# Background products of w_mod queued on VectorE behind the weight splits traced before them

## The chip, the cores and the metric

The kernel runs on one core of a Trainium2 chip, in one launch. The metric is the device time in microseconds. The engines are TensorE (PE, its weight loads PEld), VectorE (DVE), ScalarE (ACT) and SyncE (SP, here the queue that issues the transfers); GpSimd (POOL) does next to nothing. Each engine runs its own queue in order, and waits on semaphores where an instruction needs another engine's result or a transfer.

## The reference, cut to what matters

Two layers over 256 tokens of width 2048, all in float32. Each layer normalises, modulates by a vector that comes from `c`, projects, runs two mixing branches, merges them and projects back. The part that the change touches is the product of the modulation, a row times a matrix of 2048 x 6144 in each layer:

```python
c_act = jax.nn.silu(c)
...
mod = c_act @ w_mod + b_mod
shift, scale, gate = jnp.split(mod, 3, axis=-1)
h = rms_norm(x, g_norm) * (1.0 + scale[:, None, :]) + shift[:, None, :]
proj = h @ w_in
...
y_ret = (o_ret * jax.nn.silu(rg)) @ w_ret_proj
...
y_mla = (o_mla * jax.nn.silu(mg)) @ w_mla_proj
...
out = merged @ w_out
return x + gate[:, None, :] * out
```

## The kernel before, in words

**Weights.** Every weight matrix is streamed once from memory in loads of 512 KB (128 partitions x 1024). A load lands in one of five staging buffers (`wst`, pool `wp`, WP = 5; `load`, line 237, issued on SP). To keep float32 accuracy with the faster matmul, each weight is split into two parts: `split_into` lets ScalarE write the rounded part `hi` (line 241) and VectorE the rest `lo` = source minus `hi` (line 242). Both go into one of three buffers (`whl`, pool `hp`, HP = 3). `chunk` (line 264) then runs the matmuls of this load: two for each block with `hi` (line 270), and after these one with `lo` (line 273). A staging buffer is free when its split has ended; a `whl` buffer is free when the matmuls of its load have ended. `load_split` (line 246) traces load and split, the split with a priority of 200 ahead of its place (SPLITS).

**The modulation.** The product with `w_mod` runs on VectorE: for every 128 rows of `w_mod` one instruction multiplies a block of 128 x 512 by one column of `cact` and adds it to an accumulator (`mod_rows`, lines 344 and 346). It is cut into pieces of one load, thus two such instructions (a pair), and these pieces wait in the list `background`. `load_split` calls `bg()` ahead of its own load; `bg()` adds `rate` to a credit and traces a piece for each whole credit. A piece is traced in one of two ways. `mod_pair` (line 391), for the first products of a layer, loads into two buffers of its own (`ring`, RING = 2) and adds into two accumulators `tmp`; it runs from 45 to 275 us and from 1110 to 1235. `mod_slice` (line 405) loads into the weights' staging buffers and adds into `macc`; there are 64 such pieces in layer 0 (439 to 950 us) and 32 in layer 1 (1477 to 1865). The rates: 0.85 and 0.76 a load in the first products; in layer 0 then 0.6 (RB, branch products, up to 590 us), 0.3 (RM, attention, 600 to 800) and 0.5 (RG, output gates, up to 950); in layer 1 0.3 throughout (BG1). After the last piece of a block of 512 columns `mod_finish` cuts the sum into three bf16 pieces (ScalarE line 362, VectorE 363) that small matmuls add up over the partitions (line 352).

**The order of the work.** The kernel is traced in Python, and a planner gives each engine its queue when the trace is done. It goes by priority (the place in the trace, less what `high_priority` takes off) and by its own estimate of when an instruction can start. So the order on an engine is not the order of the trace: a product whose transfer the planner takes to have landed goes ahead of a split whose buffer it takes to be busy still. The names that matter are `split_into`, `load_split`, `mod_rows`, `mod_pair` and `mod_slice`.

Of the kernel before, what the change touches and what calls it, by code (L numbers as in the profile page):

```python
# [9 lines left out]
F32 = mybir.dt.float32  # L10
# [4 lines left out]
ALU = mybir.AluOpType  # L15
# [93 lines left out]
def trunk(ctx: ExitStack, tc: tile.TileContext, x, c, positions, w_mod, b_mod, g_norm, w_in, g_cq,  # L109
          g_ckv, w_uq, w_ukv, w_ret_proj, w_mla_proj, w_out, g_final, consts, decay, out):  # L110
    nc = tc.nc
    V, A, T, DMA = nc.vector, nc.scalar, nc.tensor, nc.sync
# [17 lines left out]
    def tmp_tile():  # L130
        return tp.tile([P, 512], F32, name="tmp", tag="tmp")
# [101 lines left out]
    def load(src, nk, n):  # L233

        t = wp.tile([P, 1024], F32, name="wst", tag="wst")
        v = t[:, : nk * n].rearrange("p (k n) -> p k n", k=nk)
        DMA.dma_start(v, src.rearrange("(k p) n -> p k n", p=P))
        return v

    def split_into(hi, lo, src):  # L240
        A.activation(hi, src, AF.Copy)  # L241
        V.tensor_tensor(lo, src, hi.bitcast(F32), ALU.subtract)  # L242

    prepared = []

    def load_split(src, nk, n, early=False):
        if prepared and not early:
            return prepared.pop(0)
        bg()
        w = load(src, nk, n)  # L250
        t = hp.tile([P, 2, 1024], F32R, name="whl", tag="whl")
        hi = t[:, 0, : nk * n].rearrange("p (k n) -> p k n", k=nk)
        lo = t[:, 1, : nk * n].rearrange("p (k n) -> p k n", k=nk)
        with tc.high_priority(offset=SPLITS):
            split_into(hi, lo, w)
        return hi, lo

    def mm3(o, a, b, start, stop):
# [22 lines left out]
    def proj(w, col, n, act, span=(0, KT)):  # L281
        accs = [acc_tile() for _ in range((n + 2 * P - 1) // (2 * P))]
        nk = 1024 // n
        for k0 in range(*span, nk):
            hi, lo = load_split(w[k0 * P : (k0 + nk) * P, col : col + n], nk, n)
            proj_chunk(accs, hi, lo, k0, nk, span, act)
        return accs

    def proj_tok(w, col, act, span=(0, KT)):

        accs = [acc_tile() for _ in range(2)]
        for k0 in range(*span, 2):
            hi, lo = load_split(w[k0 * P : (k0 + 2) * P, col : col + 512], 2, 512)
            chunk([(accs[t].rearrange("p a b -> p (a b)"), (hi[:, k, :], lo[:, k, :]),
                    act.block(k0 + k, slice(t * P, (t + 1) * P)), k0 + k == span[0], k0 + k == span[1] - 1, True)
                   for k in range(2) for t in range(2)])
        return [a.rearrange("p a b -> p (a b)") for a in accs]
# [41 lines left out]
    macc = cp.tile([P, 512], F32, name="macc")  # L339

    def mod_rows(acc, w, k0, nk):
        for k in range(nk):
            if k0 + k == 0:
                V.tensor_scalar(acc, w[:, k, :], cact[:, 0:1], None, ALU.mult)
            else:
                V.scalar_tensor_tensor(acc, w[:, k, :], cact[:, k0 + k : k0 + k + 1], acc, ALU.mult, ALU.add)  # L346
# [10 lines left out]
    def mod_finish(l, m0, ng, acc):  # L357

        t1, t2 = (tp.tile([P, 2, 512], BF16, name="part", tag="tmp") for _ in range(2))
        pieces = [t[:, : ng * P] for t in (t1[:, 0], t1[:, 1], t2[:, 0])]  # L360
        for i in range(2):
            A.activation(pieces[i], acc, AF.Copy)
            V.tensor_tensor(pieces[2] if i else acc, acc, pieces[i], ALU.subtract)
        if l < DEPTH - 1 or m0 < 32:
            mod_sum(l, m0, ng, pieces, ones_h[:, 0:1])
            return
        b, n = tmp_tile(), m0 - 32
        DMA.dma_start(b, b_mod[l, m0 * P : m0 * P + 512].unsqueeze(0).broadcast_to([P, 512]))
        if n % 8 == 0:
            gate_row.append(quarter("grow"))  # L370
        ps = aux_tile()
        for i, piece in enumerate(pieces):
            T.matmul(ps, ones_h, piece, start=i == 0, stop=i == 2)
        V.tensor_tensor(gate_row[n // 8][:, n % 8 * P : n % 8 * P + 512], ps, b, ALU.add)

    rings, used = [], [0]

    def ring():
        if not rings:
            rings.extend(quarter("ring") for _ in range(RING))  # L380
        return rings

    def mod_fetch(w, l, m0, k0, ng):

        n = ng * P
        w = w.rearrange("p (k n) -> p k n", n=n)
        nd = 1024 // n
        DMA.dma_start(w, w_mod[l, k0 * P : (k0 + nd) * P, m0 * P : m0 * P + n].rearrange("(k p) n -> p k n", p=P))
        return w

    def mod_pair(l, kg, ng):

        acc = [tmp_tile()[:, : ng * P] for _ in range(2)]
        nd = 8 // ng
        for k0 in range(0, KT, nd):
            for i in range(2):
                room = ring()
                used[0] += 1
                mod_rows(acc[i], mod_fetch(room[used[0] % len(room)], l, kg + 16 * i, k0, ng), k0, nd)
                yield  # L400
        for i, a in enumerate(acc):
            mod_finish(l, kg + 16 * i, ng, a)
        make_amul(l, kg, ng)

    def mod_slice(l, m0, k0):
        w = load(w_mod[l, k0 * P : (k0 + 2) * P, m0 * P : m0 * P + 512], 2, 512)
        mod_rows(macc, w, k0, 2)
        if k0 + 2 == KT:
            mod_finish(l, m0, 4, macc)

    def make_amul(l, k, n):
        V.scalar_tensor_tensor(amul[l][:, k : k + n], mods[l][:, 16 + k : 16 + k + n], 1.0,
                               gn[l][:, k : k + n], ALU.add, ALU.mult)
# [4 lines left out]
    def bg():  # L418
        credit[0] += rate[0] if background else 0
        while background and credit[0] >= 1:  # L420
            credit[0] -= 1
            background.pop(0)()
# [12 lines left out]
    def make_h(l, k, xh, hh):  # L435

        t = tmp_pair()
        for i in range(2):
            scale, shift = amul[l][:, k + i : k + i + 1], mods[l][:, k + i : k + i + 1]
            A.activation(t[:, i], xh[:, i], AF.Identity, bias=shift, scale=scale)  # L440
        split_into(*hh.pair(k // 2), t)
# [52 lines left out]
    def start():  # L494
# [8 lines left out]
        with tc.manual_schedule(engines={ENG.PE, ENG.DVE, ENG.Activation}):  # L503
# [32 lines left out]
            for k in range(ng):  # L536
                V.tensor_scalar(xh0[:, k, :], xh0[:, k, :], amul[0][:, k : k + 1], None, ALU.mult)
            first = [w_in[0, k0 * P : (k0 + 2) * P, n : n + 512] for n in (C_RQ, C_RK) for k0 in range(0, ng, 2)]
            prepared.append(load_split(first[0], 2, 512, early=True))
            mod_sum(0, 0, ng, [acc], ones[:, 0:1])  # L540
            for k in range(ng):
# [7 lines left out]
    def scaled(l, n):  # L549


        w = S + 2
        tiles = [quarter("u", F32R) for _ in range((2 * n + 2) // 3)]
        parts = [tiles[i // 3][:, i % 3 * w : (i % 3 + 1) * w] for i in range(2 * n)]
        for k in range(n):
            t = tmp_tile()[:, :w]
            V.tensor_scalar(t[:, :S], xT[:, k, :], amul[l][:, k : k + 1], None, ALU.mult)
            V.tensor_copy(t[:, S:], mods[l][:, k : k + 1].broadcast_to([P, 2]))
            split_into(parts[2 * k], parts[2 * k + 1], t)
        return parts  # L560
# [426 lines left out]
    def queue(l, lo, hi):  # L987
        for m in range(lo, hi, 4):
            for k0 in range(0, KT, 2):
                background.append(lambda l=l, m=m, k0=k0: mod_slice(l, m, k0))  # L990
# [26 lines left out]
```

## Time and profile before

| | |
|---|---|
| median of 3 runs | 2107.25 us (2105.28 to 2107.37) |
| the profiled execution | 2107.54 us, of which the span from the first to the last instruction is 2105.8 us |
| mean granted TensorE clock | 0.993 of full speed |
| TensorE matmuls busy | 97% of the span |
| VectorE busy | 72% |
| ScalarE busy | 50% |
| read from memory | 456 MB, 218 GB/s over the span with what is written |

Times in the rows below are microseconds from the span's start. A busy share is a mean over stages, so the stages are looked at one by one. A line such as `DVE macc L346` is VectorE writing the tile `macc` at line 346 of the kernel; `<-DMA wst<-in_w_mod` names what ended the idle time before it. Idle time of an engine counts only if TensorE or the end of the kernel waits for it in turn.

### The profile page before, as it was taken

The numbers are of one execution on the slowest core, as the hardware profiler recorded it, in microseconds if no ns is written. First come the engines' busy times: TensorE is split into PE (matmuls) and PEld (weight loads), VectorE is DVE, ScalarE is ACT, GpSimd is POOL, SyncE is SP. The second block draws the span as 40 slices with busy tenths as digits, with TensorE's granted clock in tenths as the row PEclk, the third lists the DMA queues.
The fourth block names the chain that finished last, engine by engine and source line by source line (L and its number), as shares of the span: only waits on it lengthen the run. The fifth ranks groups of instructions, "written<-read, shape, count | busy, mean of one in ns | idle before, by whom it ended". The sixth has DMA issues, their size and how long they took to land. (4 is left out here: it accounts for less than half of the span.)

```text
span 2105.8 us, 31895 instructions
## 1 busy us (share of the span) xinstructions
PE 2045.3 (97%) x12410; PEld 1806.7 (86%) x12414; DVE 1505.9 (72%) x2258; ACT 1060.1 (50%) x1489; POOL 0.2 (0%) x4
## 2 busy tenths in 40 slices
PE   7999999999999999999999999999999999999998
PEld 4887888997789998778999779889878999988887
DVE  5789887777777786666577776557866777765564
ACT  4554355654356665334454454446544666644453
POOL 0000000000000000000000000000000000000000
PEclk9999999999999999999999999999999999999999
DMA  8988866566766667776558976665667666666672
GB/s 315 310 283 274 293 190 199 165 196 228 263 203 194 186 196 250 242 242 216 181 167 304 313 256 184 196 186 156 196 220 231 184 193 186 216 221 189 192 243 91
DMA packets 263511, 460.60 MB, mean 219 GB/s; under 512 B 18464, under 2 KB 68032, under 8 KB 263360
## 3 DMA queue, kind: packets, MB, share of 16 engines
q1 hardware_dynamic: 263360, 458.57, 68.4%
q8 instruction: 97, 1.59, 0.3%
q14 instruction: 54, 0.44, 0.1%
HBM read 456.41 MB, written 2.10 MB: 218 GB/s over the span
## 5 line engine op out<-in xcount | busy, mean ns | idle before, releaser
L241 ACT ACTIVATE whl<-wst 128x1024 fp32r<-128x1024 f32 (+1 forms) x708 | 706.9, 1006 | 770.4 <-PE acc L273 634.9
L242 DVE TENSOR_TENSOR whl<-wst,whl 128x1024 fp32r<-128x1024 f32 (+1 forms) x708 | 811.6, 1156 | 267.2 <-ACT whl L241 264.0
L270 PE MATMUL acc<-whl,h 128*128 128x512 f32 x2048 | 513.6, 391 | 0.9 <-DVE rv L606 0.7
L270 PEld LDWEIGHTS acc<-whl,h 128*128 128x128 f32 x2048 | 381.6, 188 | 79.8 <-issue 1.7
L270 PE MATMUL acc<-h,whl 128*128 128x256 f32 x2432 | 331.0, 287 | 8.6 <-ACT h L241 3.8
L270 PEld LDWEIGHTS acc<-h,whl 128*128 128x128 f32 x2432 | 310.0, 194 | 12.5 <-ACT h L241 5.0
L273 PE MATMUL acc<-whl,h 128*128 128x512 f32 x1024 | 281.8, 395 | 8.5 <-DVE whl L242 8.1
L270 PE MATMUL acc<-whl,z 128*128 128x512 f32 x1024 | 256.7, 392 | 3.8 <-ACT whl L241 3.8
L346 DVE SCALAR_TENSOR_TENSOR macc<-wst,cact,macc 128x512 f32<-128x512 f32 x180 | 135.0, 750 | 140.9 <-DMA wst<-in_w_mod 138.8
L273 PEld LDWEIGHTS acc<-whl,h 128*128 128x128 f32 x1024 | 188.8, 188 | 53.9 <-DVE whl L242 16.9
L270 PEld LDWEIGHTS acc<-whl,z 128*128 128x128 f32 x1024 | 192.8, 189 | 44.7 <-ACT whl L241 4.5
L273 PE MATMUL acc<-h,whl 128*128 128x256 f32 x1216 | 175.1, 284 | 0.0
L273 PEld LDWEIGHTS acc<-h,whl 128*128 128x128 f32 x1216 | 159.1, 193 | 0.1
L273 PE MATMUL acc<-whl,z 128*128 128x512 f32 x512 | 139.8, 395 | 13.2 <-DVE whl L242 13.1
L346 DVE SCALAR_TENSOR_TENSOR tmp<-ring,cact,tmp 128x512 f32<-128x512 f32 x150 | 112.0, 751 | 51.4 <-DMA ring<-in_w_mod 49.9
L273 PEld LDWEIGHTS acc<-whl,z 128*128 128x128 f32 x512 | 95.2, 189 | 39.2 <-DVE whl L242 20.3
L270 PE MATMUL acc<-c,whl 128*128 128x256 f32 x640 | 102.7, 289 | 1.0 <-DVE ma L643 1.0
L270 PEld LDWEIGHTS acc<-c,whl 128*128 128x128 f32 x640 | 86.8, 191 | 1.3 <-ACT q L241 1.2
L270 PE MATMUL acc<-m,whl 128*128 128x256 f32 x512 | 67.3, 283 | 0.0
L270 PEld LDWEIGHTS acc<-m,whl 128*128 128x128 f32 x512 | 64.0, 192 | 0.1
L270 PE MATMUL acc<-whl,m 128*128 128x512 f32 (+1 forms) x256 | 56.5, 365 | 0.0
L273 PE MATMUL acc<-c,whl 128*128 128x256 f32 x320 | 56.0, 283 | 0.0
(259 smaller groups left out, 1889.7 us busy)
## 6 DMA issues: line engine op xcount, KB each, us to landing
wst<-in_w_in SPq DMA_DIRECT2D x416, 512.0 KB, 4.5
wst<-in_w_mod SPq DMA_DIRECT2D x96, 512.0 KB, 4.3
ring<-in_w_mod SPq DMA_DIRECT2D x80, 512.0 KB, 5.5
wst<-in_w_ret_proj SPq DMA_DIRECT2D x64, 512.0 KB, 4.8
wst<-in_w_mla_proj SPq DMA_DIRECT2D x64, 512.0 KB, 4.6
wst<-in_w_out SPq DMA_DIRECT2D x64, 512.0 KB, 3.7
wst<-in_w_ukv SPq DMA_DIRECT2D x32, 512.0 KB, 3.8
wst<-in_w_uq SPq DMA_DIRECT2D x32, 384.0 KB, 4.0
```

The costliest lines, as they stand in the source:

```text
L241: A.activation(hi, src, AF.Copy)
L242: V.tensor_tensor(lo, src, hi.bitcast(F32), ALU.subtract)
L270: T.matmul(o, x, y, start=start and i == 0, stop=False, skip_group_check=True)
L273: T.matmul(o, x, y, start=False, stop=stop, skip_group_check=True)
L346: V.scalar_tensor_tensor(acc, w[:, k, :], cact[:, k0 + k : k0 + k + 1], acc, ALU.mult, ALU.add)
```

## The change

`split_into` hands back its VectorE instruction, and `load_split` keeps it in the list `last_split`. `behind_splits()` gives a context in which every VectorE instruction that is traced gets an edge to the split that was traced last. The edge is an order in VectorE's queue at planning time; it is no semaphore. Both places that trace background products, `mod_pair` and `mod_slice`, trace `mod_rows` in that context. The loads of `w_mod` are outside of it, and so is `mod_finish`. The products in `start()`, at the head of the kernel, stay as they are.

```diff
--- before.py
+++ after.py
@@ -239,9 +239,13 @@
 
     def split_into(hi, lo, src):
         A.activation(hi, src, AF.Copy)
-        V.tensor_tensor(lo, src, hi.bitcast(F32), ALU.subtract)
-
-    prepared = []
+        return V.tensor_tensor(lo, src, hi.bitcast(F32), ALU.subtract)
+
+    prepared, last_split = [], []
+
+    def behind_splits():
+
+        return tc.issue_after(last_split[-1].ins) if last_split else nullcontext()
 
     def load_split(src, nk, n, early=False):
         if prepared and not early:
@@ -252,7 +256,7 @@
         hi = t[:, 0, : nk * n].rearrange("p (k n) -> p k n", k=nk)
         lo = t[:, 1, : nk * n].rearrange("p (k n) -> p k n", k=nk)
         with tc.high_priority(offset=SPLITS):
-            split_into(hi, lo, w)
+            last_split.append(split_into(hi, lo, w))
         return hi, lo
 
     def mm3(o, a, b, start, stop):
@@ -396,7 +400,9 @@
             for i in range(2):
                 room = ring()
                 used[0] += 1
-                mod_rows(acc[i], mod_fetch(room[used[0] % len(room)], l, kg + 16 * i, k0, ng), k0, nd)
+                w = mod_fetch(room[used[0] % len(room)], l, kg + 16 * i, k0, ng)
+                with behind_splits():
+                    mod_rows(acc[i], w, k0, nd)
                 yield
         for i, a in enumerate(acc):
             mod_finish(l, kg + 16 * i, ng, a)
@@ -404,7 +410,8 @@
 
     def mod_slice(l, m0, k0):
         w = load(w_mod[l, k0 * P : (k0 + 2) * P, m0 * P : m0 * P + 512], 2, 512)
-        mod_rows(macc, w, k0, 2)
+        with behind_splits():
+            mod_rows(macc, w, k0, 2)
         if k0 + 2 == KT:
             mod_finish(l, m0, 4, macc)
```

## Rows read from the trace of the kernel before

**Rows 1.** Page, part 1: engine, busy us, share of the span, instructions

```profile
PE 2045.3 (97%) x12410; PEld 1806.7 (86%) x12414; DVE 1505.9 (72%) x2258; ACT 1060.1 (50%) x1489; POOL 0.2 (0%) x4
```

**Rows 2.** Waits: who waited for whom: us in total, times, longest us

```profile
DVE macc L346 <- DMA wst<-in_w_mod: 138.8, 74, 6.3
```

**Rows 3.** Windows by stage: length, busy us (x instructions) by engine, TensorE clock, DMA

```profile
500.00:600.00 100.00, 90.47 (x453) 74.24 (x453) 72.83 (x104) 36.15 (x42) 0.00 (x0) 0.95 0.75 246
600.00:800.00 200.00, 198.91 (x1659) 197.42 (x1658) 156.01 (x308) 129.34 (x256) 0.00 (x0) 1.00 0.64 193
850.00:965.00 115.00, 105.29 (x483) 81.92 (x484) 77.30 (x93) 44.21 (x50) 0.00 (x0) 1.00 0.74 243
1610.00:1868.00 258.00, 255.97 (x1946) 246.57 (x1947) 193.73 (x356) 157.03 (x291) 0.00 (x0) 1.00 0.65 200
```

**Rows 4.** Timeline, VectorE, 865 to 877: start, us, instruction [idle before <- releaser]

```profile
865.02 2.35 DVE L242 TENSOR_TENSOR whl<-wst,whl 128x1024 fp32r<-128x1024 f32 x2
870.50 1.54 DVE L346 SCALAR_TENSOR_TENSOR macc<-wst,cact,macc 128x512 f32<-128x512 f32 x2 [3.12 <-DMA wst<-in_w_mod]
871.95 1.22 DVE L242 TENSOR_TENSOR whl<-wst,whl 128x1024 fp32r<-128x1024 f32 x1
876.06 0.75 DVE L346 SCALAR_TENSOR_TENSOR macc<-wst,cact,macc 128x512 f32<-128x512 f32 x1 [2.89 <-DMA wst<-in_w_mod]
```

**Rows 5.** Timeline, the same stretch, ScalarE and TensorE

```profile
865.73 1.06 ACT L241 ACTIVATE whl<-wst 128x1024 fp32r<-128x1024 f32 x1 [3.67 <-PE acc L273]
...
878.00 1.20 PE L273 MATMUL acc<-whl,z 128*128 128x512 f32 x4 [1.76 <-DVE whl L242]
```

**Rows 6.** Timeline, VectorE: first and last pair of macc, and their splits

```profile
445.15 0.48 DVE L344 TENSOR_SCALAR macc<-wst,cact 128x512 f32<-128x512 f32 x1
...
452.71 1.22 DVE L242 TENSOR_TENSOR whl<-wst,whl 128x1024 fp32r<-128x1024 f32 x1
...
1862.92 1.54 DVE L346 SCALAR_TENSOR_TENSOR macc<-wst,cact,macc 128x512 f32<-128x512 f32 x2 [4.31 <-DMA wst<-in_w_mod]
...
1867.86 2.35 DVE L242 TENSOR_TENSOR whl<-wst,whl 128x1024 fp32r<-128x1024 f32 x2
```

**Rows 7.** Timeline, TensorE: transposes that end an output block, layers 0 and 1

```profile
851.15 0.87 PE L895 MATMUL aux<-cst,tmp 128*128 128x128 f32 x6
...
903.28 0.88 PE L895 MATMUL aux<-cst,tmp 128*128 128x128 f32 x6
...
1967.04 0.81 PE L895 MATMUL aux<-cst,tmp 128*128 128x128 f32 x6
...
2011.47 0.82 PE L895 MATMUL aux<-cst,tmp 128*128 128x128 f32 x6
```

**Rows 8.** Timeline of VectorE, ScalarE, TensorE, 499 to 506; window 505 to 513

```profile
499.73 0.75 DVE L346 SCALAR_TENSOR_TENSOR macc<-wst,cact,macc 128x512 f32<-128x512 f32 x1 [1.43 <-DMA wst<-in_w_mod]
...
503.19 0.21 ACT L302 ACTIVATE small<-small 128x4 f32<-128x4 f32 x1 [4.07 <-DVE small L745]
...
505.34 3.78 PE L270 MATMUL acc<-whl,z 128*128 128x512 f32 x8 [3.54 <-ACT whl L241]
...
505.00:513.00 8.00, 6.05 (x14) 4.26 (x15) 7.34 (x12) 0.44 (x2) 0.00 (x0) 0.50 0.66 233
```

**Rows 9.** Waits of matmuls (PE) and weight loads (PEld), 500 to 600

```profile
PE acc L273 <- DVE whl L242: 5.0, 4, 1.6
...
PEld acc L273 <- DVE whl L242: 7.4, 6, 2.3
```

**Rows 10.** Waits of weight loads, 1477 to 1610

```profile
PEld acc L273 <- DVE whl L242: 4.4, 3, 1.8
```

**Rows 11.** Timeline, VectorE, 99 to 110: a split, the first group's last products

```profile
99.37 1.22 DVE L242 TENSOR_TENSOR whl<-wst,whl 128x1024 fp32r<-128x1024 f32 x1
...
108.72 1.54 DVE L346 SCALAR_TENSOR_TENSOR tmp<-ring,cact,tmp 128x512 f32<-128x512 f32 x2 [0.31 <-DMA ring<-in_w_mod]
```

**Rows 12.** Page, part 6: issues, KB each, median us to landing

```profile
wst<-in_w_mla_proj SPq DMA_DIRECT2D x64, 512.0 KB, 4.6
```

## The prediction

> **What bounds the kernel now.** I read the busy table first: TensorE is busy for 2045.3 of 2105.8 us, VectorE for 72%, ScalarE for 50% [rows 1]. So the kernel is as long as TensorE's work plus what TensorE waits, and a change that moves VectorE's work can only win or lose TensorE's waits. Next the list of waits: the longest wait of VectorE that isn't for a weight half of ScalarE is that of the products of w_mod (line 346) for their own transfer, 138.8 us in 74 waits [rows 2]. Then the table by stage, to find where TensorE loses: 9.5 us of 100 in the stage 500 to 600 and 9.7 of 115 in 850 to 965, but only 1.1 of 200 and 2.0 of 258 in the two attention stages [rows 3]. Those first two are the stages in which a product is traced before every second load or more (rates 0.6 and 0.5).
>
> The timeline shows the two joined. VectorE runs its queue in order. Two splits end at 867.4; next in the queue is a product of w_mod, and VectorE stands 3.12 us until that transfer has landed and runs the pair of products (1.54 us); only then, at 871.95, comes a weight split [rows 4]. The other half of that weight had been written by ScalarE at 865.73 plus 1.06, so the split could have run from 866.8: it lost 5.1 us to a product [rows 5]. The next split waits in the same way behind a product that stood 2.89 us and began at 876.06 [rows 4], and TensorE stands 1.76 us for that split until 878.00 [rows 5].
>
> Does the change reach these products? Loads go out on SP in the order in which they are traced, and the splits run in that order too, so I numbered them: for each of the 96 pairs of products that share the weights' five staging buffers I counted the splits that were traced before the pair but run after it. 92 of 96 pairs have at least one, most two or three: the first pair begins at 445.15, while the split traced last before it runs at 452.71; the last pair runs at 1862.92, its split (the first of the two merged) at 1867.86 [rows 6]. The change forbids just that.
>
> **The change, part by part.** No instruction, transfer or semaphore is added or taken away; 92 pairs of 1.54 us move behind one to three splits of 1.22 us on VectorE. The loads of w_mod keep their place on SP's queue. What follows from a move is the release of the product's staging buffer, and so the load five places on, and the loads behind that one on SP.
>
> *Stage 850 to 955* (rate 0.5). The same work runs in layer 1 without products, so I price it by the period from one set of output transposes to the next: 903.28 - 851.15 = 52.1 us here (the next period is as long), 2011.47 - 1967.04 = 44.4 us there [rows 7]. The difference is 7.7 us a period, 15.4 us in two; a part of it is the small matmuls of a finished block, which stay. A chunk of one load needs 2.72 us of TensorE (44.4 less some 0.9 for the eight transposes, over 16), and its split needs 1.22 of VectorE, the products 0.77 on the mean: once in order, nothing on VectorE is late by its length. I take 12 of 15.4, leaving some for landings that are late by themselves. A rule of the Trainium skill bears on this price: the page Perfetto Trace Analysis, section Identifying the Most-Contended Engine, says that matmul busy time is no good measure of how near to its limit TensorE is, since matmuls overlap in the trace. By busy time the stage has only 9.7 us to give; by the period 15.4. The trace agrees with the rule, as the period sets the same work with products against the same without.
>
> *Stage 500 to 600* (rate 0.6). TensorE waits 5.0 us for splits by its own idle time and 7.4 by that of the weight loads [rows 9]. Beside it stands one other wait: ScalarE stood 4.07 us until 503.19 for statistics (line 745) on VectorE, the weight copies behind it came late, and TensorE stood 3.54 us until 505.34; after it the granted clock was 0.50, the lower of its two levels (1.2 GHz), from 505 to 513 [rows 8]. TensorE is busy for 6.05 us of that stretch at half speed, so 3.0 lost. Sum 5.0 + 3.5 + 3.0 = 11.5 to 7.4 + 3.5 + 3.0 = 13.9. The product at 499.73, which stood 1.43 us for its transfer in front of those statistics [rows 8], goes behind the split it overtook, so the statistics come some 2 us sooner; whether 3.5 us shrink enough for the clock to hold is open. I take 10.
>
> *Stage 1477 to 1610* (layer 1, rate 0.3): the weight loads wait 4.4 us for splits [rows 10]. I take 3.
>
> *Attention stages* (600 to 800 and 1610 to 1868): 3.1 us of waits altogether [rows 3]. Here a pair overtakes up to five splits and moves far, so the sign is open: the gain is at most 3.1, the loss is bounded below as a rival. I take 1.5 won.
>
> *First products of each layer* (45 to 330, 1100 to 1260), where products read two buffers of their own. There most pairs already run behind the split that they will be tied to: the last of the first group is traced before load 22 (16 products at 0.85 a load are 19 calls, and three loads were prepared without one), whose predecessor's split is at 99.37, and it runs at 108.72 [rows 11]. Of 80 such pairs I count 21 that overtake a split, mostly one split by half a pair. Their stalls for their own transfers stay in the queue ahead of splits. I take 1.5, with -2 to +4 as bounds, and 0.5 for the rest.
>
> Sum: 12 + 10 + 3 + 1.5 + 1.5 + 0.5 = 28.5 us. The profiled execution took 2107.54 us (span 2105.8 and 1.7 around it), 0.3 above the median of 2107.25; 2107.5 - 28.5 = **2079 us**. If all is won the terms are 15.4 + 13.9 + 4.4 + 3.1 + 4 + 0.5 = 41.3, so 2066.
>
> **What could take the place of the wait.** *The five staging buffers bind.* A load holds a buffer from its issue to the end of its split or pair. Five buffers and 1.5 loads for each chunk allow a mean hold of 5 x 2.72 / 1.5 = 9.1 us at full speed (8.5 at rate 0.6). Now the chunk takes 52.1 / 16 = 3.26 us, hence a mean hold of 10.9. After: a landing of 4.6 us [rows 12], then 1.06 and 1.22 with 0.1 between each are 7.1 us for a weight; a pair must outlast the split before it, whose load is issued no later, so at most 7.1 + 1.5 = 8.6. Mean 7.6 to 7.7, with 0.8 to 1.5 to spare. If queues on ScalarE and VectorE add 2.5 us to each, the hold is 10.1, the chunk 3.0 us, and some 0.25 x 32 = 8 us are won in the 850 stage and 4 elsewhere: 2095 us. In its favour: a product now leaves its buffer before the weights, and will hold it longest. The same page of the Trainium skill, section Optimization Strategy, says that a gap that repeats on the engine that should be full can mean too few buffers for the next tile. By that rule an order alone would cure little, which is this rival; the trace bears it out only in part, as VectorE stood idle 3.12 us with a finished weight half before it.
>
> *Slower: the products land on the softmax chain.* In the attention stages VectorE carries the chain scores, maximum, exponent, scale, and TensorE has only 3.1 us of idle time, so what is late there is paid in full. About 29 pairs are traced there (0.3 x 48 loads in each layer). A pair put between a split and the next link of the chain costs up to 1.54 us; from 18 of 29 on, the 27 us won elsewhere are gone, and with all 29 the kernel is 45 - 27 = 18 us slower: 2125 us. Against it: VectorE is 78% busy there [rows 3], not full, the pairs stand in the same queue now, and TensorE hardly waits.
>
> *Nothing moves.* The planner orders VectorE by its own estimate of times; where a pair goes behind its split, the next split may be put behind the pair's other half as before, and the same waits come one place on. That gives 2107 within 4. Against it: by then the product's transfer has landed, since it was issued before the next weight's.
>
> **How the numbers follow.** Forecast (2066 to 2093; the half of the sum is the least that I call this case): 0.70. Buffers bind (2093 to 2106): 0.12. Slower by the chain: 0.11, between 2112 and 2128. Nothing moves: 0.07. The range of 8 in 10 is 2064 to 2104: the forecast's case, with 2 us below its end for a stall that I haven't priced, and most of the second. Faster by over 0.2% (4.2 us, about what a measurement of this kernel can tell from no change) is 0.70 and nearly all of the second, less some at its end: 0.79; within: 0.10; slower: 0.11.
>
> **What the profile will show.** If right: the waits of macc's products for DMA fall from 138.8 us to under 40; the transposes' period falls from 52.1 to 45 to 47 us; the granted clock stays at 1.00 from 505 to 513; no pair of macc overtakes a split. If the buffers bind, the period stays above 49 and ScalarE's weight copies wait for DMA. If the chain pays, the attention stages' idle time rises from 3.1 us to 20 and more. A waiting time of products for DMA that stays over 100 us would make the whole mechanism wrong.

## The result

The changed kernel takes 2076.30 us (median of 4, 2073.70 to 2077.98) where the kernel before, on the same chip, takes 2106.27 us (4 runs, 2101.77 to 2107.37): a ratio of 0.9857, 95% interval 0.9842 to 0.9872, or 30.0 us faster. Forecast were 2079 us, 28.2 below the median known then. The profiled execution of the changed kernel took 2073.70 us with a span of 2071.9; against the span of 2105.8 before that is 33.9 us, so the two traces show some 4 us more of a gain than the medians do.

Part 1 of the changed kernel's page (engine, busy us, share, instructions) answers [rows 1]:

```profile
PE 2033.4 (98%) x12413; PEld 1806.7 (87%) x12414; DVE 1511.5 (73%) x2258; ACT 1062.2 (51%) x1489; POOL 0.2 (0%) x4
```

The work is the same on every engine, to within 1% of its busy time; TensorE's share has risen since the kernel is shorter. The list of waits of the changed kernel (who waited for whom: us in total, times, longest us; line numbers are 4 higher behind the new function, so 346 is now 350 and 273 is 277):

```profile
DVE whl L242 <- ACT whl L241: 358.2, 308, 5.8
ACT whl L241 <- DMA wst<-in_w_ret_proj: 11.8, 5, 3.4
PE acc L274 <- ACT h L241: 8.0, 3, 5.5
PEld acc L277 <- DVE whl L242: 5.8, 11, 1.0
PE acc L277 <- DVE whl L242: 1.9, 5, 0.6
DVE macc L350 <- DMA wst<-in_w_mod: 0.2, 1, 0.2
```

The 138.8 us of [rows 2] are 0.2. TensorE's waits for splits, in the whole kernel before 21.1 us by its own idle time and 37.2 by that of its weight loads, are 1.9 and 5.8. VectorE is hardly busier for it: it now stands in front of splits until ScalarE has written the first half (264.0 us before, 358.2 now), and ScalarE in turn stands for TensorE. That is what an unhindered chain looks like: the engine that bounds is the one that is waited for. One wait of TensorE is clearly larger than before, that for `h` (3.8 before); it comes up again below.

The same stages as [rows 3] and the window of [rows 8] in the changed kernel, whose work stands up to 34 us earlier (length, busy us and instructions of PE, PEld, DVE, ACT, POOL, TensorE clock, DMA share, GB/s):

```profile
500.00:600.00 100.00, 98.80 (x562) 84.92 (x561) 81.30 (x117) 44.36 (x60) 0.00 (x0) 1.00 0.82 273
600.00:800.00 200.00, 199.46 (x1614) 195.57 (x1614) 156.25 (x299) 128.95 (x247) 0.00 (x0) 1.00 0.64 191
850.00:965.00 115.00, 115.00 (x538) 94.40 (x537) 79.47 (x89) 50.73 (x56) 0.00 (x0) 1.00 0.76 253
1610.00:1868.00 258.00, 257.48 (x1854) 242.97 (x1855) 191.62 (x333) 155.02 (x277) 0.00 (x0) 1.00 0.67 202
505.00:513.00 8.00, 8.00 (x51) 6.83 (x50) 7.46 (x11) 3.21 (x4) 0.00 (x0) 1.00 0.84 268
```

TensorE's idle time falls from 9.5 to 1.2 us in the stage of rate 0.6, from 9.7 to nothing in that of rate 0.5, and from 3.1 to 1.1 in the two attention stages together. VectorE's timeline in the stage of [rows 4] shows why (start, us, instruction, [idle before <- releaser]):

```profile
864.25 1.23 DVE L242 TENSOR_TENSOR whl<-wst,whl 128x1024 fp32r<-128x1024 f32 x1 [1.50 <-ACT whl L241]
865.39 1.53 DVE L350 SCALAR_TENSOR_TENSOR macc<-wst,cact,macc 128x512 f32<-128x512 f32 x2
```

The pair starts where a split ends and has no idle time before it: its transfer was there. The split waits for ScalarE alone.

**A ledger by landmarks.** A window holds other work after than before, so the sharper reading is to take one instruction and ask how much sooner it starts. The timeline of ScalarE and TensorE before, beside the rows at 503.19 [rows 8], 851.15, 903.28 and 2011.47 [rows 7]:

```profile
415.89 0.21 ACT L302 ACTIVATE small<-small 128x4 f32<-128x4 f32 x1
592.76 0.38 ACT L241 ACTIVATE q<-acc 128x256 fp32r<-128x256 f32 x1
955.46 0.87 PE L895 MATMUL aux<-cst,tmp 128*128 128x128 f32 x6
998.08 0.82 PE L895 MATMUL aux<-cst,tmp 128*128 128x128 f32 x6
1424.02 0.21 ACT L302 ACTIVATE small<-small 128x4 f32<-128x4 f32 x1
1621.00 0.38 ACT L241 ACTIVATE q<-acc 128x256 fp32r<-128x256 f32 x1
1877.38 0.82 PE L895 MATMUL aux<-cst,tmp 128*128 128x128 f32 x6
```

and the same instructions in the changed kernel:

```profile
416.36 0.21 ACT L306 ACTIVATE small<-small 128x4 f32<-128x4 f32 x1
496.62 0.20 ACT L306 ACTIVATE small<-small 128x4 f32<-128x4 f32 x1
503.06 2.12 PE L274 MATMUL acc<-whl,z 128*128 128x512 f32 x8 [1.20 <-ACT whl L241]
581.17 0.38 ACT L241 ACTIVATE q<-acc 128x256 fp32r<-128x256 f32 x1
836.44 0.82 PE L902 MATMUL aux<-cst,tmp 128*128 128x128 f32 x6
881.56 0.82 PE L902 MATMUL aux<-cst,tmp 128*128 128x128 f32 x6
926.69 0.82 PE L902 MATMUL aux<-cst,tmp 128*128 128x128 f32 x6
970.29 0.82 PE L902 MATMUL aux<-cst,tmp 128*128 128x128 f32 x6
1395.60 0.20 ACT L306 ACTIVATE small<-small 128x4 f32<-128x4 f32 x1
1588.62 0.38 ACT L241 ACTIVATE q<-acc 128x256 fp32r<-128x256 f32 x1
1844.94 0.82 PE L902 MATMUL aux<-cst,tmp 128*128 128x128 f32 x6
```

| stretch, by the landmarks before | sooner at its end, us | won in it, us |
|---|---|---|
| 0 to 416, first products of layer 0 | -0.5 | -0.5 |
| 416 to 593, rate 0.6 | 11.6 | 12.1 |
| 593 to 851, mostly attention | 14.7 | 3.1 |
| 851 to 955, rate 0.5, two periods | 28.8 | 14.1 |
| 955 to 998, no products | 27.8 | -1.0 |
| 998 to 1424, first products of layer 1 | 28.4 | 0.6 |
| 1424 to 1621, rate 0.3 | 32.4 | 4.0 |
| 1621 to 1877, attention | 32.4 | 0.0 |
| 1877 to the end | 33.9 | 1.5 |

Three quarters of the gain are in the two stages where a product is traced every second load or more; the first products give nothing.

### The profile page after: what moved, and what is told of

Its sections match the earlier page's. It is cut to its first block, busy times and chain, and to the rows that moved or that the text cites. A ratio compares the mean times of both kernels' runs of the same rounds, so it can differ in the third digit from the quotient of the medians.

```text
span 2071.9 us, 31906 instructions
## 1 busy us (share of the span) xinstructions
PE 2033.4 (98%) x12413; PEld 1806.7 (87%) x12414; DVE 1511.5 (73%) x2258; ACT 1062.2 (51%) x1489; POOL 0.2 (0%) x4
## 4 chain that ended last, share of the span: by engine, by line
PE 85%; DMA 6%; DVE 5%; issue 2%; ACT 2%; SPq 0%; ACTq 0%; DVEq 0%
PE acc L274 51%; PE acc L277 26%; DMA ring<-in_w_mod 5%; DVE whl L242 2%; DVE tmp L350 1%; DMA wmod<-in_w_mod 1%; PE aux L266 1%; PE aux L265 1%; PE aux L264 1%; ACT whl L241 1%; PE acc L265 1%; PE acc L266 1%; PE acc L264 1%; DVE extra L350 0%; PE aux L875 0%
## 5 line engine op out<-in xcount | busy, mean ns | idle before, releaser
L242 DVE TENSOR_TENSOR whl<-wst,whl 128x1024 fp32r<-128x1024 f32 (+1 forms) x708 | 814.5, 1155 | 361.8 <-ACT whl L241 358.2
L274 PE MATMUL acc<-h,whl 128*128 128x256 f32 x2432 | 330.7, 287 | 10.7 <-ACT h L241 8.0
L350 DVE SCALAR_TENSOR_TENSOR tmp<-ring,cact,tmp 128x512 f32<-128x512 f32 x150 | 111.7, 748 | 48.9 <-DMA ring<-in_w_mod 47.9
```

Of the source, the lines that this page charges most:

```text
L242: return V.tensor_tensor(lo, src, hi.bitcast(F32), ALU.subtract)
L274: T.matmul(o, x, y, start=start and i == 0, stop=False, skip_group_check=True)
```

## The experiments

The theory: a product of `macc` that stands in VectorE's queue ahead of a split, waiting for its own transfer, holds up a weight that is otherwise ready. Its rivals are that the buffers, the products' own length, or the order of the first products count for as much. Each experiment stands against the kernel before on its own chip; ratios carry 95% intervals.

**The changed kernel once more** (no edit), as the standard on the chip of the next three.

> The changed kernel once more, as the measure for the three beside it. 2076 us, 29 to 31 us below the kernel before, in every theory.

Measured: 2075.08 us against 2107.22, ratio 0.9848 (0.9834 to 0.9862).

**One half of the change at a time.** The edge in `mod_slice` alone (products of `macc`):

```diff
# in mod_pair, against the changed kernel
-                with behind_splits():
-                    mod_rows(acc[i], w, k0, nd)
+                mod_rows(acc[i], w, k0, nd)
```

> The edge is set in mod_slice alone, the pieces of mod_pair stay free. Theory (the gain comes from the pieces that share the weights' staging buffers, and what the edge wins between 100 and 250 us is given back at the group boundary of 283 us, where the products' last sums come no sooner): 2076 us, within 2 of the changed kernel, with a stall at the boundary near 287 us of some 2 us as before in place of 5.5. Rival (the first products carry a part of the gain): 2080 us or more. Second rival (the edge on the first products costs): 2072 us or less.

Measured: 2072.49 us, 0.9835 (0.9821 to 0.9848), 2.6 below the changed kernel and so just outside the 2 us of the theory. The edge in `mod_pair` alone (first products):

```diff
# in mod_slice, against the changed kernel
-        with behind_splits():
-            mod_rows(macc, w, k0, 2)
+        mod_rows(macc, w, k0, 2)
```

> The edge is set in mod_pair alone, the pieces of mod_slice stay free. Theory: within 3 us of the kernel before, 2104 to 2108, with macc's products waiting some 139 us for their transfers as before. Rival (the first products carry a part): 2095 to 2102.

Measured: 2106.88 us, 0.9997 (0.9988 to 1.0006), with the wait of [rows 2] in place, by the list of waits of this kernel:

```profile
DVE macc L350 <- DMA wst<-in_w_mod: 139.0, 75, 4.7
```

The whole gain belongs to `mod_slice`. Beside it the edge in `mod_pair` costs 2.6 us by the medians (intervals that overlap) and 1.7 by a landmark: the instruction at 415.89 before starts at 414.70 without that edge and at 416.36 with it. Where it goes shows at the end of the first products, in TensorE's timeline and the window from 288 to 292. With the edge (the changed kernel):

```profile
288.58 3.78 PE L274 MATMUL acc<-h,whl 128*128 128x256 f32 x16 [5.54 <-ACT h L241]
...
288.00:292.00 4.00, 3.42 (x16) 3.42 (x17) 1.29 (x2) 1.05 (x3) 0.00 (x0) 0.50 0.40 152
```

Without it (the edge in `mod_slice` alone):

```profile
288.53 0.51 PE L274 MATMUL acc<-h,whl 128*128 128x256 f32 x2 [0.58 <-ACT h L241]
...
288.00:292.00 4.00, 2.93 (x20) 2.52 (x21) 3.76 (x6) 1.94 (x3) 0.00 (x0) 1.00 0.53 162
```

And in the kernel before:

```profile
288.42 0.50 PE L270 MATMUL acc<-h,whl 128*128 128x256 f32 x2 [1.39 <-ACT h L241]
...
288.00:292.00 4.00, 3.13 (x13) 2.73 (x14) 3.66 (x6) 1.84 (x3) 0.00 (x0) 0.69 0.59 179
```

With the edge TensorE comes at 283.0 us (288.58 less 5.54) to the point where `h` needs the modulation, 4.9 us sooner than without it and 4.0 sooner than before, but `h` comes at 288.4 to 288.6 in all three kernels: the last products of the group are paced by their two buffers' transfers, as the third buffer below shows. So TensorE stands 5.54 us in one piece instead of here and there, and the granted clock is then 0.50, the lower level. What the edge had won before 280 us goes into that. The kernel before lost clock here too (0.69 in the same window) after a wait of 1.39 us.

**A third buffer for the first products**, with the full change, with the better half of it, and without any of it:

```diff
-RING = 2
+RING = 3
```

> The changed kernel with three buffers of their own for the first products instead of two. Theory (at the boundary near 283 us TensorE waits for the modulation, which is late because two buffers with a landing of 5.2 us each set the pace of the products): the stall of 5.5 us goes and the waits of tmp for DMA (48 us) fall below 20; 2070 to 2072 us. Rival (the sums after the last product, alternating with splits on ScalarE and VectorE, are the late part): the waits for DMA fall but the stall stays over 4 us, 2075 to 2077.

Measured with the full change: 2064.39 us, 0.9799 (0.9786 to 0.9813), 10.7 below the changed kernel, about twice what the stall had led me to expect. The waits of `tmp` for transfers fall to 6.5 us, as expected, but the stall didn't go: `h` comes 4.9 us sooner (283.65) and TensorE still stands 3.13 us for it, with a granted clock of 0.68 from 284 to 288. The rest of the gain lies in a place that the expectation had left out: by the landmarks 5.9 us are won up to 416.36 (410.44 here) and 10.0 up to 1395.60 (1385.56), so 4.1 come from the first products of layer 1.

> The kernel before, no edge, with three buffers for the first products instead of two. If the third buffer acts by itself, 10 to 11 us below the kernel before, as it did beside the edge: 2095 to 2098 us. If it only acts where the edge has taken the other stalls away: 2103 or more.

Measured without the change: 2095.17 us, 0.9951 (0.9936 to 0.9966), again some 10.8 below.

> The edge in mod_slice alone, and three buffers for the first products. If both act by themselves, 2072.5 less the 10.7 us that the third buffer won beside the full edge: 2062 us. If the edge in mod_pair helps once the buffers no longer set the pace (its stall at 283 us was the pace of the buffers): 2065 to 2068.

Measured with the edge in `mod_slice` alone: **2061.33 us**, 0.9785 (0.9769 to 0.9802), the fastest of all. The matmuls of 288.58 above in its timeline, and VectorE's wait for the first products' transfers:

```profile
283.36 2.08 PE L274 MATMUL acc<-h,whl 128*128 128x256 f32 x16
...
DVE tmp L350 <- DMA ring<-in_w_mod: 11.9, 14, 2.3
```

No stall, and 130 ns a matmul where the changed kernel needed 236. The gains add up (34.7 from the edge alone and 10.8 from the buffer alone are 45.5; together they gave 44.8), since they lie in different stages: by the landmark of 415.89 this kernel is 7.5 us sooner (408.35). It is the same fault with another cure: in the kernel before VectorE stood 49.9 us for the first products' transfers, and an edge leaves that standing (47.9 us in the changed kernel), as these transfers are late themselves.

**Do buffers explain the gaps?** A sixth staging buffer in the kernel before, and a fourth less in the changed one:

```diff
# kernel before (one large tile less makes the room)
-BIG = 31
-WP = 5
+BIG = 30
+WP = 6
```

> The kernel before, no edge, with six staging buffers in place of five (and 30 quarter tiles in place of 31, to make the room). Theory (the loss is the place of a product in VectorE's queue, ahead of splits that are ready): a sixth buffer lets each transfer start one load sooner, some 1.7 us, so a part of the 139 us of waits goes, but not the place: 2090 to 2102 us. Rival (too few buffers is the cause and the edge only eases it): 2080 us or less, as with the edge.

Measured: 2093.51 us, 0.9941 (0.9921 to 0.996). Its windows and its wait of products:

```profile
500.00:600.00 100.00, 88.98 (x455) 73.21 (x456) 72.48 (x101) 38.01 (x46) 0.00 (x0) 0.97 0.74 244
850.00:965.00 115.00, 113.82 (x521) 91.15 (x520) 79.62 (x93) 48.95 (x55) 0.00 (x0) 1.00 0.78 261
...
DVE macc L346 <- DMA wst<-in_w_mod: 132.4, 78, 4.7
```

A sixth buffer takes most of the idle time out of the stage of rate 0.5 and none out of that of rate 0.6, and the waits on VectorE hardly fall, where a part of them had been expected to go. It is worth 12.6 us where the order alone, with five buffers, is worth 30.0. The run doesn't change the buffers alone, though. The planner now lets pairs run one split further ahead: counted as in the prediction, 41 of the 96 pairs run ahead of four splits and 37 of three, where 51 ran ahead of three and 32 of two before. And 6.35 of the 11.0 us of idle time in the stage of rate 0.6 are one wait for a split (at 510.86), which stood in VectorE's queue behind products that waited for transfers and behind statistics. So the run shows what a sixth buffer brings with this planner; what it would bring in the old order was not tried.

```diff
# changed kernel
-WP = 5
+WP = 4
```

> The changed kernel with four staging buffers in place of five. By the arithmetic of buffers (mean hold of at least 7.6 us, 1.5 to 1.6 loads a chunk, so a chunk takes 2.85 us at rate 0.5 and 3.04 at 0.6 against 2.72): 4 us lost in the stage of 0.5, 13 in that of 0.6, 2093 us. Rival one (five buffers are already at their limit, real holds are longer): 2110 or more. Rival two (holds are shorter than worked out, five have much to spare): 2074 to 2080.

Measured: 2090.29 us, 0.9922 (0.9905 to 0.994). Waits, and the transposes that give the period:

```profile
ACT whl L241 <- DMA wst<-in_w_ret_proj: 52.6, 25, 4.8
...
845.73 0.82 PE L902 MATMUL aux<-cst,tmp 128*128 128x128 f32 x6
...
892.74 0.82 PE L902 MATMUL aux<-cst,tmp 128*128 128x128 f32 x6
```

This is what buffers that bind look like: ScalarE's weight copies wait for their transfers. The period is 47.0 us, 2.94 a chunk, so four buffers are held 4 x 2.94 / 1.5 = 7.8 us in the mean, an estimate that takes the buffers as the limit throughout; the prediction had put the mean at 7.6 to 7.7, from which 2093 us followed for this run. With five buffers and 2.82 us a chunk there is room for 9.4. So five don't bind, if a load needs no more than that, by 1.6 us a load.

**How far behind must a product go?** The edge in `mod_slice`, with none in `mod_pair`, to the last split but one:

```diff
-        return tc.issue_after(last_split[-1].ins) if last_split else nullcontext()
+        return tc.issue_after(last_split[-2].ins) if len(last_split) > 1 else nullcontext()
```

> The edge in mod_slice alone, but tied to the last split but one instead of the last: a pair may still overtake one split. Theory (a pair pays where its transfer lands after the split it overtakes is ready; with one split left to overtake, the transfer has mostly landed): most of the gain, 2076 to 2090 us, with waits of macc's products for DMA between 10 and 60 us. Rival (every overtaking costs its 1.5 us, or the edge must be strict): 2092 or more. The full edge in mod_slice took 2072.5.

Measured: 2079.01 us, 0.9878 (0.9852 to 0.9905). Its waits:

```profile
DVE macc L350 <- DMA wst<-in_w_mod: 21.5, 20, 2.6
PE aux L840 <- ACT qkn L830: 5.1, 2, 2.5
```

One split overtaken leaves 21.5 us of waits and most of the gain: the idle time of the stages 500 to 600 and 850 to 965 is 1.1 us and nothing. Most of what it lacks against the edge in `mod_slice` alone stands in attention (6.0 us of idle time in the two stages, 1.1 in the changed kernel), where TensorE twice stands 2.5 us for a link of the softmax chain.

**Is it the wait or the products' own time?** Three kernels in which the products of `macc` read a table that lies in place (`cos_t`) instead of `w_mod`. First with the transfers of `w_mod` still issued, against the kernel before:

```diff
         w = load(w_mod[l, k0 * P : (k0 + 2) * P, m0 * P : m0 * P + 512], 2, 512)
-        mod_rows(macc, w, k0, 2)
+        mod_rows(macc, cos_t.rearrange("p a b -> p (a b)").unsqueeze(1).broadcast_to([P, 2, 2 * S]), k0, 2)
```

> The kernel before, no edge, but the products of mod_slice read a table that is always in place instead of the loaded piece of w_mod; the transfers of w_mod go on as before, and the modulation's values are others. So the same products run, in whatever place the planner gives them, and none waits for a transfer. Theory (what costs is the wait for the transfer at the head of the queue): nearly all of the gain comes, 2074 to 2082 us. Rival (what costs is the products' own 1.5 us ahead of a split): 2092 us or more.

Measured: 2109.94 us, 1.002 (1.0006 to 1.0034), 28 us above the upper end of what was expected. Its waits, SP's queue and the matmuls' among them:

```profile
SPq L237 <- DMA wst<-in_w_mod: 394.4, 96, 6.2
ACT whl L241 <- DMA wst<-in_w_ret_proj: 37.7, 17, 5.0
PE acc L270 <- ACT whl L241: 13.7, 11, 2.7
PE aux L352 <- DVE extra L346: 9.7, 1, 9.7
PE acc L273 <- DVE whl L242: 1.7, 5, 0.6
```

VectorE's wait is gone and the splits are in time (1.7 us, 21.1 before). But a buffer that nobody reads is handed on as its transfer lands, and it is SP that waits for that, 394.4 us in 96 waits (99.8 in 54 before), with the loads of weights behind it in the queue. A part of the wait had moved from one queue in order to another. Beside it the products themselves had moved: free of the transfer, the first pair runs at 24.83 us, TensorE stands 9.7 us for VectorE's products of the head (2.0 before), and the two attention stages lose 8.1 us (3.1 before). So the run doesn't tell the rivals apart; it shows a second place where this fault can sit. Then without the transfers:

```diff
-        w = load(w_mod[l, k0 * P : (k0 + 2) * P, m0 * P : m0 * P + 512], 2, 512)
+        w = cos_t.rearrange("p a b -> p (a b)").unsqueeze(1).broadcast_to([P, 2, 2 * S])
         mod_rows(macc, w, k0, 2)
```

> The kernel before, no edge; the products of mod_slice read a table that is always in place, and their pieces of w_mod are not loaded at all (96 transfers of 512 KB less, the modulation's values are others). So VectorE has the same instructions, where the planner puts them, and neither VectorE nor SP waits for a piece of w_mod. Theory (the waits for those transfers at the head of a queue cost, the products' own time does not): 2065 to 2078 us. Rival (the products' own 1.5 us ahead of splits cost): 2090 us or more.

Measured: 2093.64 us, 0.9943 (0.9923 to 0.9964), in the total 16 us above the upper end of what was expected and within the range of the rival. By stage, and one wait:

```profile
500.00:600.00 100.00, 98.85 (x529) 83.25 (x529) 85.78 (x119) 42.70 (x50) 0.00 (x0) 1.00 0.57 182
850.00:965.00 115.00, 115.00 (x548) 95.23 (x546) 84.92 (x100) 51.50 (x57) 0.00 (x0) 1.00 0.60 188
1610.00:1868.00 258.00, 252.56 (x1869) 241.75 (x1871) 185.35 (x336) 154.49 (x282) 0.00 (x0) 0.99 0.55 159
...
PE aux L352 <- DVE extra L346: 8.6, 1, 8.6
```

The two stages lose 1.2 us and nothing, as the theory has it. Products that wait for nothing are free to go anywhere, though, here in the same order as in the run before: the planner puts the first at 24.69 us, so that at 44.66 TensorE stands 8.6 us for VectorE's products of the head (2.0 before), and others into attention, which now loses 5.4 us of 258 (2.0 before) and 2.7 of 200 (1.1 before). What the transfers alone cost in SP's queue is then the difference of the two runs, some 16 us (2109.94 to 2093.64, with the kernel before at 2106.14 and 2105.94 on their chips). To hold them near their place, the same with an edge to the last split but two, which lets a pair run ahead of the last two splits:

```diff
# against the run above
-        mod_rows(macc, w, k0, 2)
+        with behind_splits():    # to last_split[-3]
+            mod_rows(macc, w, k0, 2)
```

> As the run without the pieces of w_mod (products of mod_slice read a table in place, 96 transfers less, the modulation's values are others), but each pair is tied to the last split but two, so that it can't run off to the head of the kernel and overtakes two splits, as most pairs of the kernel before do. Theory (the overtaking costs only by the wait for the transfer): the stages 500 to 600 and 850 to 965 lose no more than 2 us each by TensorE's idle time, 2068 to 2080 us in all. Rival (two overtaken splits and 1.5 us of products ahead of them cost by themselves): those stages lose 5 us or more each, 2090 us or more.

Measured: 2071.38 us, 0.9839 (0.9818 to 0.9861). By stage:

```profile
500.00:600.00 100.00, 97.66 (x559) 84.23 (x558) 78.94 (x117) 44.02 (x60) 0.00 (x0) 1.00 0.55 175
850.00:965.00 115.00, 115.00 (x548) 95.30 (x547) 78.11 (x89) 50.69 (x55) 0.00 (x0) 1.00 0.60 189
```

The first stage loses 2.3 us, a little over the 2 of the theory and under the 5 of the rival, the second nothing; 74 of the 96 pairs run ahead of two splits. So a pair ahead of two splits costs next to nothing if it has nothing to wait for. The kernel before, whose pairs run ahead of two or three and wait for their transfers, is 35 us slower on this chip. One reservation: these two kernels move 96 transfers less, and their five staging buffers hold weights alone, so they bound the price of the products' own time and say nothing on the traffic or the buffers.

## Why the prediction was right, step by step

**The bound and the mechanism** hold. The order on VectorE was the cause: the half of the change that touches `macc` brings the whole gain, the wait of [rows 2] falls to 0.2 us (forecast under 40), and only 3 of the 96 pairs still run ahead of a split that was traced before them, against 92. The splits that those 3 run ahead of are splits of `w_uq`, which don't pass through `load_split`, so "no pair" was a little too strict.

**Stage 850 to 955**, forecast 12 of 15.4: 14.1 won, the period being 45.1 (forecast 45 to 47). The difference of 0.7 to the period of layer 1 is all that the small matmuls and late landings take. The Trainium skill, page Perfetto Trace Analysis, section Identifying the Most-Contended Engine, had warned that matmul busy time misjudges TensorE; the trace agrees, for by busy time the stage had 9.7 us to give and it gave 14.1.

**Stage 500 to 600**, forecast 10 of 11.5 to 13.9: 12.1 won from 416 to 593. The part that was open came out well: ScalarE's instruction of 503.19 starts at 496.62 with no wait, 6.6 us sooner where some 2 had been forecast, TensorE stands 1.20 us there instead of 3.54, and the clock stays at 1.00 from 505 to 513.

**1477 to 1610**, forecast 3 of 4.4: 4.0. **Attention**, forecast 1.5 of 3.1: by the landmarks 3.1 in layer 0 and nothing in layer 1. The windows place it otherwise: idle time falls from 1.1 to 0.5 us in layer 0 and from 2.0 to 0.5 in layer 1, 2.0 together, so most of the 3.1 between 593 and 851 isn't attention. In each of these I had taken less than the ceiling for mishaps that didn't come; against the sum of 28.5 the traces' gain of 33.9 has 2.1, 2.1, 1.0 and 1.6 more in these four terms and 1.0 more at the end, less 1.4 in the first products and 1.0 between 955 and 998. By the medians the gain is only 1.5 above the sum. That nearness is in part luck: the terms, read one by one from the traces, miss by 5.4 together, and the medians lie some 4 us closer than the traces do.

**The first products**, forecast 1.5 within -2 to 4: the term that failed, though not its bounds. Won were 0.1 us by the landmarks (-0.5 and 0.6), 0.3 by the run with that edge alone (0.9997, no change within its interval), and beside the other edge some 2 were lost (2.6 by medians whose intervals overlap, 1.7 by a landmark). The prediction had rightly said that their stalls for their own transfers stay; what it missed is what happens at the end of the group, where TensorE's gain turns into one wait of 5.54 us and a slower clock.

**The buffers' rival** (0.12) fell: ScalarE's copies of `w_ret_proj` wait 11.8 us for transfers in the changed kernel, less than before (15.8) and far from the 52.6 of four buffers; the period is below 49, and the run with one buffer less showed both the sign of binding buffers and its price. The same page of the Trainium skill, section Optimization Strategy, takes a repeating gap as a possible sign of too few buffers. A sixth buffer did shorten the gaps of rate 0.5, so the rule isn't idle here; but the traces show another cause for most of them, as the order alone removed them with five.

**The softmax rival** (0.11) fell too: 1.1 us of idle time in the attention stages where 20 and more would have shown it. It exists in small: 2.5 us twice with the edge one split shorter, and the 5.4 and 2.7 us of attention where the products were free. Why the shorter edge lands on the chain and the full one doesn't is open. **Nothing moves** (0.07) fell with the wait.

## What to carry to other kernels

In a queue that runs in order, background work that waits for its transfer in front of ready work holds that work up, whether the queue is VectorE's or the one that issues transfers. What it costs is only what the bounding engine waits in turn: here 138.8 us of waits on VectorE cost some 30 us, and the 40.7 us of them in the attention stages at most the 3.1 us that TensorE stood idle there. Look for a long wait of work that nobody needs yet, and compare when the next instruction was ready with when it ran. Tie such work behind the last critical instruction rather than leave it to the planner's estimate, and keep it tied when it waits for nothing, or a planner like this one lets it wander. Where its transfers are late themselves an edge can't help, but a buffer more for that stream can, and whether buffers bind is worked out beforehand from their number, the period and the mean hold.

## What the runs showed of the hardware that I had not expected

- The price of a TensorE stall is not its length alone. After 5.54 us the granted clock was 0.50 from 288 to 292 us and matmuls of 130 ns took 236; after waits of 0.58 and 1.20 us it was 1.00. Before the change a stall of 3.54 us was followed by 0.50 [rows 8]. Here, gathering small stalls into one took back all that had been won. The length doesn't settle it either: the kernel with the edge one split shorter has two waits of 2.53 us, the one at 664.73 followed by a clock of 0.51 (to 668.0), the one at 1727.24 by 1.00 (to 1731.0); and a wait of 1.48 us at 123.65 before the change was followed by 0.51 (125.6 to 129.1), the same wait of 1.47 at 124.14 after it by 1.00 (124 to 128).
- SP's queue stands for a buffer without a reader: 394.4 us in 96 waits, one for each such transfer, where 99.8 in 54 had been.
